# One decoder layer: the first input chunk in fp32, the decay as a background job, and a turned order of the down projection

## The chip, the cores and the metric

The kernel runs on one core of a Trainium2 chip. The metric is the device time of one execution in microseconds (us), smaller is better. The engines are TensorE (PE, matmuls; PEld is its load of weights), VectorE (DVE), ScalarE (ACT), GpSimd (POOL) and SyncE (SP), which issues most DMAs. Each engine works through its own instruction stream in order; streams meet at semaphores.

## The reference, cut to what matters

One layer of a hybrid decoder on 256 tokens of width 2048, all in float32:

```python
h = rms_norm(x, ln1)
proj = h @ w_in              # gdn q|k|v, beta, decay, z, moba q|k|v, gate a, gate b
y_a = gated_deltanet(...) @ w_branch_a     # conv of 4, silu, delta rule with decay, * silu(z)
y_b = moba_attention(rope(q_b), rope(k_b), v_b) @ w_branch_b
x = x + (sigmoid(gate_a) * y_a + sigmoid(gate_b) * y_b) @ w_out
u = causal_dwconv(rms_norm(x, ln2) @ w_up, ffn_conv, bias)
x = x + (silu(u_gate) * u_val) @ w_down
return rms_norm(x, final_norm)
```

The decay is `g = -exp(a_log) * softplus(a_logit + dt_bias)`, cumulated along the tokens for each of 8 heads; `beta` is a sigmoid of its own column. `rms_norm` is `x * rsqrt(mean(x^2)) * ln1`. The kernel leaves out the factor of the token (`rsqrt`, in the kernel `R1`) until after the matmul, since it is constant over the contraction, and multiplies only `ln1` in beforehand.

## The kernel before, in words

**Matmuls in split form.** Most matmuls take operands in fp32r. A float32 operand is split into a high part (`wh`, `hh`: a cast on ACT, line 118) and a low part (`wl`, `hl`: the rest, a subtraction on DVE, line 115), and three products are summed: high by high, high by low, low by high. `fetch` gets a raw block of 128x2048 weights by DMA into one of four buffers `wraw`; `load_w` splits it in pieces of 1024 columns into `wh` and `wl`, two buffers each. `chunk` computes two 128-row blocks of a projection against all tokens in a tile `ps` of PSUM (`mmt`, three buffers, tag "mm"); `by_token` computes the transposed form, tokens on the partitions, with 512 columns to a matmul, in two such tiles. Small things use another five PSUM buffers (`sdt`, tag "sd").

**The start.** `xs`, the transposed input, and the first two weight blocks `wq` come in 16 pieces of 256 KB, `xs` before `wq` in each pair (lines 250 and 251). For each quarter of the contraction, `scaled` multiplies `xs` by `ln1` and splits it into `hc` (`hh` on ACT, line 216; `hl` on DVE, line 217), the weights are split, and 4 x 3 matmuls for each of two blocks go to `ps_q0`: 96 in all. Then follow the fetches of `wbd`, `bd`, the second chunk's weights `raws` and the constant tables, the squares of `xs` (three of four on POOL), the 32 matmuls `ps_bd` for beta and decay, and `rstd`, which gives `R1` from a sum over the partitions by two fp32 matmuls with `ones` (tile `R`).

**The decay.** From `ps_bd` and `R1` a chain of some 25 small instructions on 16 partitions (lines 310 to 349, DVE with ACT's sigmoid and exp between) makes `beta`, the cumulated decay `gc`, its split and `rem`. `columns` transposes these and `R1` on PE into `pt_cols` and copies them to `cols`.

**The loop over groups.** For four groups of two heads, three chunks (q, k, v) are computed, and each goes through `conv4`: `join` multiplies `ps` by `R1` on DVE (line 212), which frees the PSUM tile, then come the four taps of the convolution and a silu. Groups 0 and 2 also compute `ps_z` for four heads by token. Then the group's `gdn` generator is appended to `bg`. Four groups of attention follow (`moba`), then the gates, the two branch projections, the output projection, the up projection in 44 chunks (`ps_up`) and the down projection.

**Order.** `main_mm` adds 108 to a counter for a matmul of 256 columns and 215 for one of 512; whenever it has reached `EVERY` = 1700, `tick` advances each generator in `bg` by one step. So background work is written between the main matmuls. A planner with a simulated timeline then sets the order of each engine's instructions: what is written first has priority, but work that it expects to be ready earlier can go ahead. After the third group of attention, `bg` is ticked until one job is left, and the pool `g` of the delta rule is closed.

**The down projection.** Eight PSUM banks `pd[i][n]` collect 128 tokens x 512 columns each; they take the banks that the up projection's tiles held. For each of 40 blocks of the contraction the eight are visited in `order`; the first visit begins with four transposes of `x1` (line 814). The last four blocks are done accumulator by accumulator, each followed by the final norm.

Of the kernel before, what the change touches and what calls it, by code (L numbers as in the profile page):

```python
# [11 lines left out]
F32 = mybir.dt.float32  # L12
# [68 lines left out]
def layer_kernel(ctx: ExitStack, tc: tile.TileContext, xT, pos, cst, csel, ceye, vec, convw, ffw, bdv,  # L81
# [30 lines left out]
            tick()  # L112

    def low(hi, lo, src, eng=None):
        (eng or dve).tensor_tensor(lo, src, hi.bitcast(F32), op=ALU.subtract)  # L115

    def split(hi, lo, src):
        act.copy(hi, src)  # L118
        low(hi, lo, src)

    def three(ah, al, bh, bl):
        return [(ah, bh), (ah, bl), (al, bh)]

    def fetch(src, n=2048):
        raw = wpool.tile([P, 2048], F32, name="wraw", tag="wraw", bufs=4)
# [3 lines left out]
    def parts(o=0):  # L129

        return [wpool.tile([P, 2048 + 128], F32R, name=t, tag=t)[:, o:o + 2048] for t in ("wh", "wl")]

    def load_w(src, n=2048, into=None, piece=1024, raw=None):
        raw = raw or fetch(src, n)
        wh, wl = into or parts()
        for o in range(0, n, piece):
            split(wh[:, o:o + piece], wl[:, o:o + piece], raw[:, o:o + piece])
        return wh[:, :n], wl[:, :n]


# [98 lines left out]

    xs = g.tile([P, KD, T], F32, name="xs")  # L240

    wq = []
    for b in range(2):
        raw = wpool.tile([P, 2048], F32, name="wraw", tag="wraw", bufs=4)
        wq.append((raw, *parts()))
    for i in range(4):
        s = slice(4 * i, 4 * i + 4)
        for b in range(2):
            h = slice(4 * i + 2 * b, 4 * i + 2 * b + 2)
            sp.dma_start(xs[:, h, :], xT[:, h, :])  # L250
            sp.dma_start(wq[b][0][:, 512 * i:512 * i + 512], w_gdn[b][:, 512 * i:512 * i + 512])
    ps_q0 = mmt("ps_gdn")
    for i in range(4):
        scaled(xs[:, 4 * i:4 * i + 4, :], ln1v, 4 * i, hh, hl)
        for b in range(2):
# [55 lines left out]
    dve.tensor_tensor(z0, z0, R1[:16, :], op=ALU.mult)
    act.activation(beta, z0, AF.Sigmoid)
    dve.tensor_scalar(z0, z0, bd[:, 0:1], None, op0=ALU.add)
    nz = g.tile([16, T], F32, name="nz")
    dve.scalar_tensor_tensor(nz, z0, -1.0, z0, op0=ALU.mult, op1=ALU.min)
    ez = g.tile([16, T], F32, name="ez")
    act.activation(ez, nz, AF.Exp)
    ea = fk.tile([16, 1], F32, name="ea")
    act.activation(ea, bd[:, 1:2], AF.Exp)
    den = g.tile([16, T], F32, name="den")  # L320
    dve.tensor_scalar(den, ez, 2.0, None, op0=ALU.add)
    dve.reciprocal(den, den)
    sv = g.tile([16, T], F32, name="sv")
    dve.tensor_tensor(sv, ez, den, op=ALU.mult)
    s2 = g.tile([16, T], F32, name="s2")
    dve.tensor_tensor(s2, sv, sv, op=ALU.mult)
    pv = g.tile([16, T], F32, name="pv")
    dve.tensor_scalar(pv, s2, 1.0 / 15, None, op0=ALU.mult)
    for n in (13, 11, 9, 7, 5, 3):
        dve.scalar_tensor_tensor(pv, pv, 1.0 / n, s2, op0=ALU.add, op1=ALU.mult)  # L330
    dve.scalar_tensor_tensor(pv, pv, 1.0, sv, op0=ALU.add, op1=ALU.mult)
    spv = g.tile([16, T], F32, name="spv")
    dve.tensor_scalar(spv, z0, 0.0, None, op0=ALU.max)
    dve.scalar_tensor_tensor(spv, pv, 2.0, spv, op0=ALU.mult, op1=ALU.add)
    gt = g.tile([16, T], F32, name="gt")
    dve.tensor_scalar(gt, spv, ea, -1.0, op0=ALU.mult, op1=ALU.mult)
    gc = fk.tile([16, T], F32, name="gc")
    for i in range(2):
        dve.tensor_tensor_scan(gc[:, i * P:(i + 1) * P], ones[:16, :], gt[:, i * P:(i + 1) * P], 0.0,
                               op0=ALU.mult, op1=ALU.add)  # L340
    gch = fk.tile([16, T], F32R, name="gch")
    gcl = fk.tile([16, T], F32R, name="gcl")
    split(gch, gcl, gc)
    selr = fk.tile([16, 8, P], F32R, name="selr")
    dve.tensor_copy(selr, self_)
    sint = fk.tile([48, T], F32, name="sint")
    cost = fk.tile([48, T], F32, name="cost")
    rem = cost[:16, :P]
    dve.tensor_scalar(rem, gc[:, :P], gc[:, P - 1:P], -1.0, op0=ALU.subtract, op1=ALU.mult)
    n1.close()  # L350

    ya = fk.tile([P, H, T], F32, name="ya")
# [58 lines left out]
        dve.tensor_scalar(cost, cost, -2.0, 1.0, op0=ALU.mult, op1=ALU.add)  # L411


    def columns():
# [4 lines left out]
        pe.transpose(pt[:, 32:48], rem, ident[:16, :16])  # L419
        for i in range(2):  # L420
            pe.transpose(pt[:, 80 + 16 * i:96 + 16 * i], R1[:16, i * P:(i + 1) * P], ident[:16, :16])
        cols = fk.tile([P, 7, 16], F32, name="cols")
        dve.tensor_copy(cols.rearrange("p a b -> p (a b)"), pt[:, :112])
        return cols

    def conv4(t, ps, b0):
        un = g.tile([P, 2, T], F32, name="un", bufs=1)
# [180 lines left out]
    def pair(w, i):  # L608
        return [w[2 * i], w[2 * i + 1]]

    for gr in range(4):
        h0 = 2 * gr
        kq = g.tile([P, 2, 2, T], F32, name="kq", bufs=1)
        v = g.tile([P, 2, T], F32, name="v", bufs=1)
        for a, t in enumerate((kq[:, 1], kq[:, 0], v)):
            if gr == a == 0:
                ps = ps_q0
            else:
                ps = chunk(pair(w_gdn, 3 * gr + a), hc, KD, "gdn", *([raws] if (gr, a) == (0, 1) else []))
# [57 lines left out]
    for gr in range(4):  # L677
        h0 = 2 * gr
        qk = []
        for a in range(2):  # L680
            ps = chunk(pair(w_moba, 2 * gr + a), hc, KD, "moba")
            t = m.tile([P, 2, T], F32, name=f"qk{a}")
            join(t, ps, R1b)
            qk.append(t)
        if gr % 2 == 0:
            ps = by_token(w_mv[2 * gr:2 * gr + 4], hc, KD, "ps_v")
            v4 = m.tile([P, 2, 2 * T], F32, name="v_")
            for i in range(2):
                act.mul(v4[:, i, :], ps[i], cols[:, 5 + i, 0:1])
        v = v4[:, :, (gr % 2) * T:(gr % 2 + 1) * T]  # L690
        bg.append(moba(h0, *qk, v))
        if gr == 2:
            while len(bg) > 1:
                tick()
            gdn_st.close()
            y_st = ExitStack()
            gp = y_st.enter_context(tc.tile_pool(name="gp", bufs=1, side="right", reuse_waits="tile"))


    gts = gp.tile([P, 2, 8, 512], F32, name="gts")  # L700
# [232 lines left out]
```

## Time and profile before

| | |
|---|---|
| device time, median of 3 runs | 1508.7 us (1507.93 to 1508.71) |
| profiled execution, device time | 1508.24 us |
| its span, first to last instruction | 1506.5 us |
| PE busy | 1482.6 us (98%), 8507 matmuls |
| PEld busy | 1305.9 us (87%) |
| DVE busy | 991.3 us (66%) |
| ACT busy | 743.4 us (49%) |
| POOL busy | 172.4 us (11%) |
| the chain that ended last | PE 92%, DVE 4%, ACT 1%, DMA 1% |
| DMA | 276.84 MB, mean 184 GB/s |

The span is the time between the first and the last instruction on the chip; the device time holds 1.74 us more around it. "Busy" is the time in which at least one instruction of an engine was running, as the profiler records it; a matmul's recorded length includes its way through the array, so successive matmuls overlap, and the pace of PE is read from the distance between their starts. An fp32 matmul is recorded as two matmuls.

### The profile page before, as it was taken

The numbers are of one execution on the slowest core, as the hardware profiler recorded it, in microseconds if no ns is written. First come the engines' busy times: TensorE is split into PE (matmuls) and PEld (weight loads), VectorE is DVE, ScalarE is ACT, GpSimd is POOL, SyncE is SP. The second block draws the span as 40 slices with busy tenths as digits, with TensorE's granted clock in tenths as the row PEclk, the third lists the DMA queues.
The fourth block names the chain that finished last, engine by engine and source line by source line (L and its number), as shares of the span: only waits on it lengthen the run. The fifth ranks groups of instructions, "written<-read, shape, count | busy, mean of one in ns | idle before, by whom it ended". The sixth has DMA issues, their size and how long they took to land.

```text
span 1506.5 us, 21027 instructions
## 1 busy us (share of the span) xinstructions
PE 1482.6 (98%) x8507; PEld 1305.9 (87%) x8507; DVE 991.3 (66%) x1413; ACT 743.4 (49%) x997; POOL 172.4 (11%) x130
## 2 busy tenths in 40 slices
PE   7999999999999999999999999999999999999997
PEld 7899899998988888888888888888888888888886
DVE  8888668796655444666667677676776765555554
ACT  5565454435474444434455555554555554444444
POOL 3011001141203000000101212112111120000000
PEclk9999999999999999999999999999999999999999
DMA  8355444444445555546555555555555544555552
GB/s 312 141 198 190 163 154 157 149 169 147 154 154 174 193 194 194 193 177 249 186 208 196 184 188 188 196 196 182 188 189 196 196 177 162 195 195 194 195 196 84
DMA packets 43329, 276.84 MB, mean 184 GB/s; under 512 B 5248, under 2 KB 6736, under 8 KB 11104
## 3 DMA queue, kind: packets, MB, share of 16 engines
q1 hardware_dynamic: 41408, 270.98, 50.2%
q0 software_dynamic: 960, 2.36, 0.5%
q10 hardware_dynamic: 864, 2.16, 0.4%
q8 instruction: 66, 1.08, 0.3%
q14 instruction: 31, 0.25, 0.0%
HBM read 271.68 MB, written 3.80 MB: 183 GB/s over the span
## 4 chain that ended last, share of the span: by engine, by line
PE 92%; DVE 4%; ACT 1%; DMA 1%; issue 1%; SPq 0%; DVEq 0%; ACTq 0%; POOLq 0%
PE ps_up L108 32%; PE pd L96 16%; PE ps_gate L108 10%; PE ps_gdn L108 9%; PE ps_wo L108 6%; PE ps_br L108 6%; PE ps_moba L108 3%; PE ps_z L108 3%; PE ps_v L108 3%; DVE wl L115 2%; ACT wh L118 1%; DMA xs<-in_xT 1%; PE g L96 1%; PE pu L564 1%; PE py L558 1%
## 5 line engine op out<-in xcount | busy, mean ns | idle before, releaser
L115 DVE TENSOR_TENSOR wl<-wraw,wh 128x1024 fp32r<-128x1024 f32 (+1 forms) x504 | 603.3, 1233 | 275.4 <-ACT wh L118 274.8
L118 ACT CAST wh<-wraw 128x1024 fp32r<-128x1024 f32 (+1 forms) x504 | 500.1, 1039 | 411.3 <-PE ps_up L108 117.3
L108 PE MATMUL ps_up<-h,wh 128*128 128x512 f32 x1408 | 488.6, 390 | 0.0
L108 PE MATMUL ps_up<-h,wl 128*128 128x256 f32 x1408 | 397.0, 282 | 0.0
L108 PEld LDWEIGHTS ps_up<-h,wh 128*128 128x128 f32 x1408 | 264.2, 188 | 55.4
L108 PEld LDWEIGHTS ps_up<-h,wl 128*128 128x128 f32 x1408 | 266.1, 189 | 0.1
L108 PE MATMUL ps_gate<-wh,hc 128*128 128x512 f32 x512 | 156.0, 391 | 0.0
L108 PE MATMUL ps_gdn<-hc,wh 128*128 128x256 f32 x768 | 142.5, 287 | 8.8 <-ACT wh L118 6.0
L96 PE MATMUL pd<-wl,ah 128*128 128x512 f32 x336 | 130.8, 389 | 0.0
L96 PE MATMUL pd<-wh,al 128*128 128x512 f32 x336 | 130.8, 389 | 0.0
L108 PEld LDWEIGHTS ps_gdn<-hc,wh 128*128 128x128 f32 x768 | 121.7, 194 | 9.9 <-ACT wh L118 6.0
L800 POOL TENSOR_TENSOR acts<-sg,cvf 128x256 f32<-128x256 f32 x44 | 80.7, 1833 | 423.4 <-ACT sg L799 423.4
L108 PEld LDWEIGHTS ps_gate<-wh,hc 128*128 128x128 f32 x512 | 95.8, 188 | 19.7
L108 PE MATMUL ps_gdn<-hc,wl 128*128 128x256 f32 x384 | 110.2, 287 | 1.1 <-DVE wl L115 1.1
L794 ACT ACTIVATE cvf<-unf,ffv 128x256 f32<-128x256 f32 x88 | 48.2, 595 | 104.4 <-DVE unf L212 104.4
L796 DVE SCALAR_TENSOR_TENSOR cvf<-unf,ffv,cvf 128x254 f32<-128x254 f32 (+1 forms) x176 | 77.3, 480 | 32.1 <-ACT cvf L794 31.8
L108 PE MATMUL ps_gate<-wl,hc 128*128 128x512 f32 x256 | 97.1, 391 | 0.0
L108 PE MATMUL ps_moba<-hc,wh 128*128 128x256 f32 x512 | 93.1, 282 | 0.0
L96 PE MATMUL pd<-wh,ah 128*128 128x512 f32 x336 | 92.8, 391 | 0.0
L108 PE MATMUL ps_wo<-mc,wh 128*128 128x512 f32 x256 | 89.0, 390 | 0.4 <-ACT wh L118 0.4
L118 ACT CAST ah<-acts 128x256 fp32r<-128x256 f32 x44 | 17.9, 406 | 128.0 <-PE pd L96 118.3
L108 PEld LDWEIGHTS ps_moba<-hc,wh 128*128 128x128 f32 x512 | 78.7, 188 | 0.2
(420 smaller groups left out, 1881.5 us busy)
## 6 DMA issues: line engine op xcount, KB each, us to landing
wraw<-in_w_up SPq DMA_DIRECT2D x88, 1024.0 KB, 4.8
wraw<-in_w_dn SPq DMA_DIRECT2D x44, 1024.0 KB, 4.8
wraw<-in_w_gate SPq DMA_DIRECT2D x32, 1024.0 KB, 4.8
wraw<-in_w_gdn SPq DMA_DIRECT2D x22, 1024.0 KB, 4.9
wraw<-in_w_moba SPq DMA_DIRECT2D x16, 1024.0 KB, 5.0
wraw<-in_w_o SPq DMA_DIRECT2D x16, 1024.0 KB, 4.8
wraw<-in_w_z SPq DMA_DIRECT2D x8, 1024.0 KB, 4.8
wraw<-in_w_mv SPq DMA_DIRECT2D x8, 1024.0 KB, 4.8
```

Of the source, the lines that this page charges most:

```text
L96: pe.matmul(ps, a, b, start=(start and i == 0), stop=(stop and i == n - 1), **kw)
L108: pe.matmul(ps, a, b, start=start, stop=stop, skip_group_check=True)
L115: (eng or dve).tensor_tensor(lo, src, hi.bitcast(F32), op=ALU.subtract)
L118: act.copy(hi, src)
L558: pe.matmul(py[:, p], ats[p], Tm[:, p], start=True, stop=True)
L564: pe.matmul(pu[:, p], Y[:, p, :], odd(U)[:, p], start=True, stop=True)
L794: act.activation(t[:, j, :], un[:, j, :], AF.Identity, scale=w[:, 2:3], bias=w[:, 3:4])
L796: dve.scalar_tensor_tensor(t[:, j, d:], un[:, j, :T - d], w[:, 2 - d:3 - d], t[:, j, d:], op0=ALU.mult, op1=ALU.add)
L800: pool.tensor_tensor(acts[:, c, :], sg, t[:, 1, :], op=ALU.mult)
```

## The change

The start fetches weights before `xs` in each pair. The first chunk is no longer split: the raw weights are multiplied in place by `ln1` on DVE and multiplied with the raw `xs` in fp32, 32 matmuls (not counted by `main_mm`). Ten fp32 matmuls on `ones` stand ahead of everything on PE. `scaled` still makes `hc`, now for the second chunk on, and the second chunk is written directly behind it, before the squares, `ps_bd` and `R1`. All four squares are on ACT, their sums on DVE. The decay's chain becomes a generator `decay`, appended to `bg` behind the second chunk's `conv4` and finished before `gdn(0)` starts; `R1`'s columns get transposes of their own. The pool of the delta rule is closed after the attention loop, once the last `gdn` is done. In the down projection the pairs of accumulators are visited in another order.

```diff
     def low(hi, lo, src, eng=None):
-        (eng or dve).tensor_tensor(lo, src, hi.bitcast(F32), op=ALU.subtract)
+        return (eng or dve).tensor_tensor(lo, src, hi.bitcast(F32), op=ALU.subtract)
...
-            split(wh[:, o:o + piece], wl[:, o:o + piece], raw[:, o:o + piece])
+            lows.append(split(wh[:, o:o + piece], wl[:, o:o + piece], raw[:, o:o + piece]))
...
+    warm = sdt("warm")
+    for i in range(10):
+        pe.matmul(warm[:, :P], ones, ones, start=True, stop=True)
+    wq = [wpool.tile([P, 2048], F32, name="wraw", tag="wraw", bufs=4) for _ in range(2)]
+    for i in range(4):
+        for b in range(2):
+            h = slice(4 * i + 2 * b, 4 * i + 2 * b + 2)
+            sp.dma_start(wq[b][:, 512 * i:512 * i + 512], w_gdn[b][:, 512 * i:512 * i + 512])
+            sp.dma_start(xs[:, h, :], xT[:, h, :])
+    ps_q0 = mmt("ps_gdn")
     for i in range(4):
         s = slice(4 * i, 4 * i + 4)
         for b in range(2):
-            h = slice(4 * i + 2 * b, 4 * i + 2 * b + 2)
-            sp.dma_start(xs[:, h, :], xT[:, h, :])
-            sp.dma_start(wq[b][0][:, 512 * i:512 * i + 512], w_gdn[b][:, 512 * i:512 * i + 512])
-    ps_q0 = mmt("ps_gdn")
+            w = r3(wq[b], P)[:, s]
+            dve.tensor_tensor(w, w, ln1v[:, s, None].to_broadcast([P, 4, P]), op=ALU.mult)
+        for b in range(2):
+            for k in range(4 * i, 4 * i + 4):
+                pe.matmul(ps_q0[:, b], r3(wq[b], P)[:, k], xs[:, k], start=(k == b == 0), stop=(k == KD - 1),
+                          skip_group_check=True)
     for i in range(4):
         scaled(xs[:, 4 * i:4 * i + 4, :], ln1v, 4 * i, hh, hl)
-        for b in range(2):
-            raw, wh, wl = (t[:, 512 * i:512 * i + 512] for t in wq[b])
-            split(wh, wl, raw)
-            for k in range(4):
-                a = 4 * i + k
-                main_mm(ps_q0[:, b], r3(wh, P)[:, k], hh[:, a], a == b == 0, False)
-                main_mm(ps_q0[:, b], r3(wh, P)[:, k], hl[:, a], False, False)
-                main_mm(ps_q0[:, b], r3(wl, P)[:, k], hh[:, a], False, a == KD - 1)
+    raws = [fetch(w) for w in (w_gdn[2], w_gdn[3])]
     wbd = g.tile([P, KD, 16], F32, name="wbd")
     sp.dma_start(wbd, w_bd)
     bd = fk.tile([16, 2], F32, name="bd")
     sp.dma_start(bd, bdv)
-    raws = [fetch(w) for w in (w_gdn[2], w_gdn[3])]
...
+    ps_k0 = chunk([w_gdn[2], w_gdn[3]], hc, KD, "gdn", raws)
...
-        if i < 3:
-            pool.tensor_tensor(sq[i], xv, xv, op=ALU.mult)
-        else:
-            act.activation(sq[i], xv, AF.Square)
-    pool.tensor_tensor(sq[0], sq[0], sq[1], op=ALU.add)
-    dve.tensor_tensor(sq[2], sq[2], sq[3], op=ALU.add)
+        act.activation(sq[i], xs[:, 4 * i:4 * i + 4, :], AF.Square)
+    dve.tensor_tensor(sq[0], sq[0], sq[1], op=ALU.add)
+    with tc.issue_after(lows[2].ins):
+        dve.tensor_tensor(sq[2], sq[2], sq[3], op=ALU.add)
...
+    def decay():          # the former lines 311 to 349, with tiles in buffers of pool m
+        ...               # z0 * R1, sigmoid, + bias, min
+        yield
+        ...               # exp, reciprocal
+        yield
+        ...               # the series
+        yield
+        ...               # softplus, gt, two scans to gc
+        yield
+        split(gch, gcl, gc)
+        dve.tensor_scalar(rem, gc[:, :P], gc[:, P - 1:P], -1.0, op0=ALU.subtract, op1=ALU.mult)
+        yield from wait(2)
         pt = sdt("pt_cols")
...
+    def rms_columns():
+        pt = sdt("pt_rms")
         for i in range(2):
-            pe.transpose(pt[:, 80 + 16 * i:96 + 16 * i], R1[:16, i * P:(i + 1) * P], ident[:16, :16])
+            pe.transpose(pt[:, 16 * i:16 * i + 16], R1[:16, i * P:(i + 1) * P], ident[:16, :16])
...
+            if gr == 0 and a < 2:
+                ps = (ps_q0, ps_k0)[a]
             else:
...
             conv4(t, ps, 8 * a + h0)
+            if gr == 0 and a == 1:
+                bg.append(decay())
         if gr == 0:
-            cols = columns()
+            rms_columns()
...
-        bg.append(gdn(h0, kq, v))
+        while gr == 0 and bg:
+            tick()
+        gdns.append(gdn(h0, kq, v))
+        bg.append(gdns[-1])
...
-        if gr == 2:
-            while len(bg) > 1:
-                tick()
-            gdn_st.close()
+    while gdns[-1] in bg:
+        tick()
+    gdn_st.close()
...
-    order = [(1, 2), (1, 3)] + [(0, n) for n in range(4)] + [(1, 0), (1, 1)]
+    order = [(1, 2), (1, 3), (0, 2), (0, 3), (1, 0), (1, 1), (0, 0), (0, 1)]
```

## Rows read from the trace of the kernel before

**Rows 1.** The waits of PE: instruction, releaser, us in total, times, longest.

```profile
PE ps_gdn L108 <- ACT wh L118: 6.0, 1, 6.0
...
PE pd L814 <- DVE unf L210: 1.7, 1, 1.7
...
PE u L570 <- DVE U L565: 0.8, 1, 0.8
...
PE pT L662 <- DVE s__4149 L656: 0.4, 1, 0.4
```

**Rows 2.** The chain of waits in order: start us, us, engine, tile, line, count.

```profile
27.65 3.74 PE ps_bd L96 x32
31.75 0.86 PE R L96 x4
32.61 21.95 PE ps_gdn L108 x188
...
61.59 5.72 PE ps_z L108 x24
67.31 0.79 PE ssq L460 x8
```

**Rows 3.** The timeline, PE's start: start us, us, instruction, idle before.

```profile
9.40 0.63 PE L108 MATMUL ps_gdn<-hc,wh 128*128 128x256 f32 x2
...
9.83 0.41 PE L108 MATMUL ps_gdn<-hc,wl 128*128 128x256 f32 x1
...
16.40 0.58 PE L108 MATMUL ps_gdn<-hc,wh 128*128 128x256 f32 x1 [1.88 <-DVE hc L217]
```

**Rows 4.** Stretches of PE: from:to, length, busy, count, granted clock, DMA share, GB/s.

```profile
6.00:12.70 6.70, 6.02 (x25) 1.00 0.99 319
...
16.10:22.90 6.80, 5.42 (x23) 0.50 1.00 379
```

**Rows 5.** The timeline, DVE and ACT, 11 to 30 us.

```profile
11.73 4.62 DVE L217 SCALAR_TENSOR_TENSOR hc<-xs,vc,hc 128x256 fp32r<-128x256 f32 x2
...
22.75 0.87 DVE L217 SCALAR_TENSOR_TENSOR hc<-xs,vc,hc 128x256 fp32r<-128x256 f32 x2
...
24.68 0.68 DVE L115 TENSOR_TENSOR wl<-wraw,wh 128x512 fp32r<-128x512 f32 x1
...
27.25 1.23 DVE L115 TENSOR_TENSOR wl<-wraw,wh 128x1024 fp32r<-128x1024 f32 x1 [0.42 <-ACT wh L118]
...
26.17 3.90 ACT L118 CAST wh<-wraw 128x1024 fp32r<-128x1024 f32 x4 [6.23 <-PE ps_gdn L108]
```

**Rows 6.** The timeline, ACT and the DMA issues on SP.

```profile
8.81 0.62 ACT L118 CAST wh<-wraw 128x512 fp32r<-128x512 f32 x1 [1.44 <-DMA wraw<-in_w_gdn]
...
11.67 0.33 SPq L251 DMA_DIRECT2D wraw<-in_w_gdn  x1
...
14.50 0.34 SPq L126 DMA_DIRECT2D wraw<-in_w_gdn  x1
```

**Rows 7.** DMA issues at 11.67 and at 14.50: count, KB, us to landing.

```profile
wraw<-in_w_gdn SPq DMA_DIRECT2D x1, 256.0 KB, 6.1
...
wraw<-in_w_gdn SPq DMA_DIRECT2D x1, 1024.0 KB, 6.2
```

**Rows 8.** The timeline, the decay's chain: its first step and `pt_cols`.

```profile
35.40 0.41 DVE L311 TENSOR_TENSOR z<-z,R 16x256 f32<-16x256 f32 x1
...
54.59 0.23 PE L417 MATMUL pt_cols<-ct,gc 16*128 16x16 f32 x1
```

**Rows 9.** The timeline, PE in `ps_z`.

```profile
61.59 0.70 PE L108 MATMUL ps_z<-wh,hc 128*128 128x512 f32 x2 [0.72 <-DVE un L212]
```

**Rows 10.** The timeline, the first pass of the down projection.

```profile
1256.35 0.68 DVE L210 TENSOR_TENSOR unf<-ps_up,unf 128x512 f32<-128x512 f32 x1
...
1257.09 0.66 PE L814 MATMUL pd<-identb,x 128*128 128x128 f32 x4 [1.74 <-DVE unf L210]
...
1258.28 0.60 PE L814 MATMUL pd<-identb,x 128*128 128x128 f32 x4
```

More of the change, by code (lines that the diff above doesn't have):

```diff
@@ L114, in low @@
     def low(hi, lo, src, eng=None):
-        (eng or dve).tensor_tensor(lo, src, hi.bitcast(F32), op=ALU.subtract)
+        return (eng or dve).tensor_tensor(lo, src, hi.bitcast(F32), op=ALU.subtract)
     def split(hi, lo, src):
         act.copy(hi, src)
-        low(hi, lo, src)
+        return low(hi, lo, src)
     def three(ah, al, bh, bl):
         return [(ah, bh), (ah, bl), (al, bh)]
+    lows = []
     def fetch(src, n=2048):
@@ L240, in layer_kernel @@
     xs = g.tile([P, KD, T], F32, name="xs")
-    wq = []
-    for b in range(2):
-        raw = wpool.tile([P, 2048], F32, name="wraw", tag="wraw", bufs=4)
-        wq.append((raw, *parts()))
+    warm = sdt("warm")
[8 more added lines that the diff above has]
+    ps_q0 = mmt("ps_gdn")
     for i in range(4):
@@ L307, in layer_kernel @@
     beta = fk.tile([16, T], F32, name="beta")
-    z0 = g.tile([16, T], F32, name="z0")
+    sint = fk.tile([48, T], F32, name="sint")
+    z0 = sint[:16]
     act.copy(z0, s[32:48, :])
     dve.tensor_tensor(z0, z0, s[:16, :], op=ALU.add)
[L311 to L317, printed above, removed]
-    ea = fk.tile([16, 1], F32, name="ea")
[L319 to L336, printed above, removed]
+    ea = fk.tile([16, 1], F32, name="ea")
     gc = fk.tile([16, T], F32, name="gc")
-    for i in range(2):
-        dve.tensor_tensor_scan(gc[:, i * P:(i + 1) * P], ones[:16, :], gt[:, i * P:(i + 1) * P], 0.0,
-                               op0=ALU.mult, op1=ALU.add)
     gch = fk.tile([16, T], F32R, name="gch")
     gcl = fk.tile([16, T], F32R, name="gcl")
-    split(gch, gcl, gc)
     selr = fk.tile([16, 8, P], F32R, name="selr")
     dve.tensor_copy(selr, self_)
-    sint = fk.tile([48, T], F32, name="sint")
     cost = fk.tile([48, T], F32, name="cost")
     rem = cost[:16, :P]
-    dve.tensor_scalar(rem, gc[:, :P], gc[:, P - 1:P], -1.0, op0=ALU.subtract, op1=ALU.mult)
+    cols = fk.tile([P, 7, 16], F32, name="cols")
     n1.close()
@@ L411, in rotary @@
         dve.tensor_scalar(cost, cost, -2.0, 1.0, op0=ALU.mult, op1=ALU.add)
-    def columns():
+    def decay():
+        nz, ez, den, sv, s2, pv, spv, gt = (m.tile([16, T], F32, name=n, tag=t) for n, t in (
+            ("nz", "qk0"), ("ez", "qk0"), ("den", "qk1"), ("sv", "qk1"), ("s2", "s_"), ("pv", "s_"),
+            ("spv", "pT_"), ("gt", "pT_")))
+        dve.tensor_tensor(z0, z0, R1[:16, :], op=ALU.mult)
+        act.activation(beta, z0, AF.Sigmoid)
+        dve.tensor_scalar(z0, z0, bd[:, 0:1], None, op0=ALU.add)
+        dve.scalar_tensor_tensor(nz, z0, -1.0, z0, op0=ALU.mult, op1=ALU.min)
+        yield
+        act.activation(ez, nz, AF.Exp)
+        act.activation(ea, bd[:, 1:2], AF.Exp)
+        dve.tensor_scalar(den, ez, 2.0, None, op0=ALU.add)
+        dve.reciprocal(den, den)
+        dve.tensor_tensor(sv, ez, den, op=ALU.mult)
+        dve.tensor_tensor(s2, sv, sv, op=ALU.mult)
+        yield
+        dve.tensor_scalar(pv, s2, 1.0 / 15, None, op0=ALU.mult)
+        for n in (13, 11, 9, 7, 5, 3):
+            dve.scalar_tensor_tensor(pv, pv, 1.0 / n, s2, op0=ALU.add, op1=ALU.mult)
+        dve.scalar_tensor_tensor(pv, pv, 1.0, sv, op0=ALU.add, op1=ALU.mult)
+        yield
+        dve.tensor_scalar(spv, z0, 0.0, None, op0=ALU.max)
+        dve.scalar_tensor_tensor(spv, pv, 2.0, spv, op0=ALU.mult, op1=ALU.add)
+        dve.tensor_scalar(gt, spv, ea, -1.0, op0=ALU.mult, op1=ALU.mult)
+        for i in range(2):
+            dve.tensor_tensor_scan(gc[:, i * P:(i + 1) * P], ones[:16, :], gt[:, i * P:(i + 1) * P], 0.0,
+                                   op0=ALU.mult, op1=ALU.add)
+        yield
+        split(gch, gcl, gc)
+        dve.tensor_scalar(rem, gc[:, :P], gc[:, P - 1:P], -1.0, op0=ALU.subtract, op1=ALU.mult)
+        yield from wait(2)
         pt = sdt("pt_cols")
@@ L419, in columns @@
         pe.transpose(pt[:, 32:48], rem, ident[:16, :16])
+        dve.tensor_copy(cols[:, :5].rearrange("p a b -> p (a b)"), pt[:, :80])
+    def rms_columns():
+        pt = sdt("pt_rms")
         for i in range(2):
-            pe.transpose(pt[:, 80 + 16 * i:96 + 16 * i], R1[:16, i * P:(i + 1) * P], ident[:16, :16])
-        cols = fk.tile([P, 7, 16], F32, name="cols")
-        dve.tensor_copy(cols.rearrange("p a b -> p (a b)"), pt[:, :112])
-        return cols
+            pe.transpose(pt[:, 16 * i:16 * i + 16], R1[:16, i * P:(i + 1) * P], ident[:16, :16])
+        dve.tensor_copy(cols[:, 5:].rearrange("p a b -> p (a b)"), pt[:, :32])
     def conv4(t, ps, b0):
@@ L609, in pair @@
         return [w[2 * i], w[2 * i + 1]]
+    gdns = []
     for gr in range(4):
@@ L615, in layer_kernel @@
         for a, t in enumerate((kq[:, 1], kq[:, 0], v)):
-            if gr == a == 0:
-                ps = ps_q0
+            if gr == 0 and a < 2:
+                ps = (ps_q0, ps_k0)[a]
             else:
-                ps = chunk(pair(w_gdn, 3 * gr + a), hc, KD, "gdn", *([raws] if (gr, a) == (0, 1) else []))
+                ps = chunk(pair(w_gdn, 3 * gr + a), hc, KD, "gdn")
             conv4(t, ps, 8 * a + h0)
+            if gr == 0 and a == 1:
+                bg.append(decay())
         if gr == 0:
-            cols = columns()
+            rms_columns()
         if gr % 2 == 0:
@@ L691, in layer_kernel @@
         bg.append(moba(h0, *qk, v))
-        if gr == 2:
-            while len(bg) > 1:
-                tick()
-            gdn_st.close()
-            y_st = ExitStack()
-            gp = y_st.enter_context(tc.tile_pool(name="gp", bufs=1, side="right", reuse_waits="tile"))
+    while gdns[-1] in bg:
+        tick()
+    gdn_st.close()
+    y_st = ExitStack()
+    gp = y_st.enter_context(tc.tile_pool(name="gp", bufs=1, side="right", reuse_waits="tile"))
     gts = gp.tile([P, 2, 8, 512], F32, name="gts")
```

2 lines of the change are left out of this document (removed).

## The prediction

> **What bounds the kernel now.** I read the page first, then the list of what TensorE (PE) waited for, the chain of waits, and the timeline of the few places that these two name. On the page the reader is to see that PE is busy almost all of the span and that the chain that ended last is nearly all PE. So a step pays only where it changes the start or the end of the unbroken PE stream, closes one of the stream's holes, or changes its matmuls. The list of PE's waits [rows 1] shows how few holes there are: 6.0 us at the very start, 1.7 us at the first transposes of the down projection (`pd`), 0.7 us in `ps_z` [rows 9], and six others of 0.4 to 0.8 us (0.8 + 0.7 + 0.7 + 0.5 + 0.4 + 0.4 = 3.5 us). The chain [rows 2] shows the start: the first chunk's matmuls last to 27.65, the 32 matmuls of `ps_bd` and the sum of `R` follow, and from 32.61 the next chunks stand back to back.
>
> How the first 27.65 us pass is in the timeline. No matmul before 5.97. Then matmuls of 256 columns are spaced 0.215 us (two in 0.43, 9.40 to 9.83 [rows 3]), where 188 of them take 21.95 us, 0.117 each, later [rows 2]. A ratio of nearly two is the clock: PE runs at 1.2 GHz there and at 2.4 GHz later. The granted clock stands at 1.00 for 6 to 12.7 us and at 0.50 for 16.1 to 22.9 [rows 4]; for the first of the two I go by the spacing. At 16.40 PE had stood 1.88 us for `hc` [rows 3], behind VectorE (DVE), whose two scalings of `xs` took 4.62 us where two take 0.87 otherwise [rows 5]; GpSimd was busy with squares of `xs` in that stretch.
>
> [...] By the recorded grant PE would be at full clock from its first matmul, the ten added matmuls would raise nothing, and the start would be worth 5.0 us; by the spacing it is 4.6.
>
> **The first chunk.** Removed: 96 matmuls on split operands, eight casts on ScalarE (ACT) and eight subtractions on DVE for the split. Added: eight scalings on DVE of 128x512, for which the subtraction of the same shape stands (0.68 us, [rows 5]), and 32 matmuls in fp32 of 256 columns. Their price is in `R`: its first sum is two such matmuls, recorded as four, in 0.86 us [rows 2], so 0.43 us each at full clock, 0.86 at the low one. The 32 cost 13.8 us against 96 x 0.117 = 11.2: 2.6 us more work for PE, which the waits must pay for.
>
> When can they run? The 16 pieces of 256 KB keep their number; each pair is swapped, so weights take the `xs` places. The fourth piece was in at 8.81, which ended an ACT wait of 1.44 us; the last landed 6.1 us after its issue at 11.67, at 17.8 [rows 6, 7]. After the change the fourth piece is `xs` of blocks 2 and 3, and the program needs it for the third matmul. So PE does two matmuls on arrival (about 5.3), stands until 8.8, and has 30 left: 30 x 0.43 = 12.9, to 21.7 at best. From there PE is slower than the data (17.8 plus one scaling of 0.7).
>
> The clock is the unknown. The ten fp32 matmuls on `ones` have 128 columns, half of `R`'s, so 0.43 us each at the low clock: 4.3 us, about 1.0 to 5.3, ahead of any data, at no cost. But the pause before 8.8 follows, 2 us or more, like the one of 1.88 us before 16.40, and after that one the grant was 0.50 [rows 3, 4]. Best case: full clock from 8.8, end at 21.7. Worst likely case: PE slow from 8.8 as long as it was from 16.4 to 22.9 [rows 3, 4], 6.5 us, half of it lost: 25.0. I take 23.0, nearer the best, since PE has worked 6 us before the pause and works on without a hole after it.
>
> The second chunk must be ready then. Its first raw block, issued at 14.50, landed 6.2 us later, at 20.7 [rows 6, 7]; it now goes ahead of `wbd`, so 20.3 to 20.7. One cast (four in 3.90 us, so 1.0) and one subtraction (1.23) [rows 5] give the first half at 22.6 to 22.9. Its other input, `hc`, needs 16 scalings on DVE (0.44 each, 7.0 us), which with the eight new ones make 12.5 us of DVE from 4.3 on, and GpSimd's squares, which stretched them, are gone to ACT (four of about 1.0 us, in idle ACT). So the second chunk begins at 23.0 in the place of 27.65: a gain of 4.6 us, bounds 2.6 (25.0) and 5.0 (22.6). `ps_bd` and `R` (27.65 to 32.61, 4.96 us) only move behind this chunk and cost the same. The fetches of `raws` pass `wbd` and `bd` on SP's queue; both small tables are wanted only after the second chunk. The third chunk's weights need the slots of the first, free at 23.0, where the last of its subtractions began at 24.68 [rows 5]: no later.
>
> **Decay as a background job.** Before, the joins of the first three chunks stood behind the decay's chain on DVE: `z0` times `R1` at 35.40, `pt_cols` at 54.59 [rows 8], and the second join let `ps_z` wait 0.72 us at 61.59 [rows 9]. Afterwards the joins need `R1` alone. `R` ends near 23.0 + 11.2 + 5.0 = 39.2, `R1` is usable 2.8 us later as before (32.61 to 35.40), at 42.0, and the third chunk runs to 39.2 + 11.2 = 50.4. Two joins and one set of taps take some 5 us of DVE, so `ps_z` finds its buffers free: gain 0.7, bounds 0 and 0.7. The decay's own instructions are the same; ACT may load a table or two more, which is idle time there. I add 0.5 us, bounds 0 and 2, for holes that DVE's new order may leave in front of a split of weights.
>
> **Turned order of the down projection.** PE finishes two accumulators and then stands 1.74 us for `pd0_0`, whose bank the last chunk's join still reads (1256.35, [rows 10]). Turned, this pair comes last: six accumulators 1.2 us apart (1257.09 to 1258.28) stand before it, four more than now, 4.8 us of cover for 1.7 of wait. The pairs put before it take the banks of the last chunk but one and but two, joined a chunk earlier and more. Gain 1.7, bounds 0 (if the planner holds the join still longer) and 1.7. The closing of the pool for the branch A work moves behind the loop; its last job had ended before the old place by my count of ticks (48 of some 49), so nothing.
>
> **Sum.** 1508.24 (profiled execution) - 4.6 - 0.7 + 0.5 - 1.7 = 1501.7. That execution is 0.46 under the median of 1508.7 and inside the runs' spread, so 1501.7 stands for the median too. The likeliest case's own range: gains of 5.0 + 0.7 + 1.7 with no new hole give 1500.8; 2.6 + 0 + 1.7 less 1 give 1504.9.
>
> **Rivals.**
> *DVE bunches its work.* If its order puts the 16 scalings of `xs` behind the last scaling of weights (18.5), they end at 25.5 and the subtraction at 26.7; the second chunk starts there, gain 0.95 in place of 4.6: 1505.4. For it: DVE is the busiest engine beside PE at the start. Against: in the trace it alternates the two kinds piece by piece.
>
> *`pt_cols` in the middle of `ps_z` (slower).* The decay's job sends its transposes to PE at its seventh step. By the tick count (1700 units, 108 a matmul of 256 columns, 215 of 512) that is 7 matmuls of 0.24 us (24 in 5.72, [rows 2]) into `ps_z`: 50.4 + 1.7 = 52.1. The decay's chain took 54.59 - 35.40 = 19.2 us; from 42.0 it ends at 61.2. If PE's order follows the code, PE stands 9.1 us: 1510.8. It decides from the point where the transposes stand within 4.3 us of `ps_z`'s start (18 matmuls): then the whole gain is gone. Against: the planner places work by when it expects it ready; `gdn`'s `ssq`, written after all of `ps_z`, ran inside it (67.31, [rows 2]).
>
> *The clock stays down.* If the whole first chunk runs at 1.2 GHz, 30 x 0.86 = 25.8 from 8.8 is 34.6, 7.0 later than before: 1513.3. It loses from an end of the chunk at 29.6 on. Against: PE had full clock after 6.7 us of work with only short holes before [rows 4].
>
> *Other holes close too.* The six others go with the new interleaving: 1501.7 - 3.5 = 1498.2. They could as well grow.
>
> **Chances.** Forecast 0.66, bunched DVE 0.14, `pt_cols` 0.06, clock 0.04, other holes 0.10. Range 1497.5 to 1506.0: it leaves out the two slow rivals, part of the bunched case and the tail below, 0.18 in all. 0.2% is 3.0 us, about what can be told from no change: faster means under 1505.7. Forecast, closed holes and two thirds of the bunched case: 0.85 faster. The rest of that and half of the `pt_cols` case: 0.08 same. Slower 0.07.
>
> **What would show it.** The first chunk as 64 records ending near 23; the second chunk from there without a hole; `ps_z` without its wait; `pd` without its 1.7 us; the later stretches of the same length. It is wrong if PE's stretch of matmuls at the low clock reaches far past 12, if DVE's last scaling of `xs` lies after 21, or if PE waits for `pt_cols`.

## The result and the profile after

The changed kernel takes 1498.91 us (median of 4, 1497.78 to 1499.27) against 1508.32 for the kernel before (median of 4 beside it): a ratio of 0.9935, 95% interval 0.9923 to 0.9947. The forecast was 1501.7, with 1497.5 to 1506.0 as its range. The gain, 9.4 us, is larger than the 6.5 to 7 forecast.

The page of the profiled execution, its span, PE's line and the granted clock in 40 slices:

```profile
span 1497.3 us, 20988 instructions
...
PE 1485.1 (99%) x8495; PEld 1308.3 (87%) x8495; DVE 986.6 (66%) x1415; ACT 738.6 (49%) x990; POOL 164.3 (11%) x126
...
PEclk9999999999999999999999999999999999999999
```

PE is busy 2.5 us longer than before in a span 9.2 us shorter. Of the 2.5 us, 2.0 are not there when the changed kernel is run again (1483.1 us): the first profile has a stretch at the low clock, told of at the end. The fp32 matmuls are a little more work, and the holes are fewer. What PE waited for, in full (instruction, releaser, us in total, times, longest), answers to [rows 1]:

```profile
PE warm L247 <- POOL ones L147: 1.0, 1, 1.0
PE ps_gdn L108 <- DVE wl L115: 0.7, 1, 0.7
PE ps_wo L108 <- DVE wl L115: 0.7, 1, 0.7
PE ps_v L108 <- DVE wl L115: 0.6, 1, 0.6
PE ps_wo L108 <- ACT wh L118: 0.4, 1, 0.4
PE ps_gdn L264 <- DMA xs<-in_xT: 0.4, 1, 0.4
PE ps_gate L108 <- DVE qk L214: 0.3, 1, 0.3
```

The 6.0 us at the start, the wait of `ps_z`, the two of `u` and those of `pT` are gone, and so is the 1.7 us of `pd`. The start on PE's timeline, to be held against [rows 3]:

```profile
1.00 4.63 PE L247 MATMUL warm<-ones 128*128 128x128 f32 x20 [1.00 <-POOL ones L147]
5.70 1.68 PE L264 MATMUL ps_gdn<-xs,wraw 128*128 128x256 f32 x4
7.73 13.22 PE L264 MATMUL ps_gdn<-xs,wraw 128*128 128x256 f32 x60 [0.35 <-DMA xs<-in_xT]
20.64 0.55 PE L108 MATMUL ps_gdn<-hc,wh 128*128 128x256 f32 x2
21.90 0.38 PE L108 MATMUL ps_gdn<-hc,wl 128*128 128x256 f32 x1 [0.72 <-DVE wl L115]
```

The ten warm matmuls (20 records) fill the time before data. The fp32 matmuls start at 5.70, with four records in 1.68 us. They stand 0.35 us for the second piece of `xs`, and run on at 0.22 us a record from 7.73, at full clock. From 20.64 on the second chunk is ready but for its low part: the 0.72 us at 21.90. Where that comes from is on ACT's and DVE's timeline, where [rows 5] stood:

```profile
17.88 1.67 DVE L219 SCALAR_TENSOR_TENSOR hc<-xs,vc,hc 128x256 fp32r<-128x256 f32 x4
...
19.54 1.99 ACT L118 CAST wh<-wraw 128x1024 fp32r<-128x1024 f32 x2 [0.63 <-DMA wraw<-in_w_gdn]
...
20.62 2.36 DVE L115 TENSOR_TENSOR wl<-wraw,wh 128x1024 fp32r<-128x1024 f32 x2 [1.08 <-ACT wh L118]
```

The cast waits 0.63 us for the raw block to land, the subtraction for the cast, PE for the subtraction. DVE had been done with `xs` for 1.1 us. From 21.90 the chain runs without a break through what stands in [rows 2] and on through `ps_z`:

```profile
21.90 11.23 PE ps_gdn L108 x94
33.13 3.63 PE ps_bd L96 x32
36.76 0.86 PE R L96 x4
37.62 11.20 PE ps_gdn L108 x96
49.05 21.99 PE ps_z L108 x96
```

For the comparison of runs, the first `ps_z` matmul marks the end of the start. Read off PE's timelines, in us:

| kernel | first `ps_z` | from there to first `ps_br` | first to last matmul of `pd` | median, runs |
|---|---|---|---|---|
| before | 55.14 | 526.78 | 245.13 | 1508.32, 4 |
| changed, first profile | 48.98 | 525.77 * | 243.16 | 1498.91, 4 |
| changed, run again | 49.22 | 524.16 | 243.15 | 1497.67, 5 |
| changed, old order in `pd` | 49.19 | 524.18 | 245.13 | 1499.69, 5 |
| changed, no warm matmuls | 49.20 | 524.15 | 243.15 | 1499.49, 5 |
| changed, split first chunk | 51.09 | 524.87 | 243.15 | 1499.59, 5 |
| changed, decay at once | 48.79 | 524.30 | 243.15 | 1497.44, 5 |
| changed, old closing of the pool | 48.78 | 525.75 * | 243.16 | 1498.88, 5 |
| changed, squares on GpSimd | 56.72 | 524.13 | 243.15 | 1503.29, 5 |
| changed, second chunk late | 50.18 | 524.22 | 243.15 | 1498.57, 5 |
| changed, raw blocks in halves | 48.47 | 524.24 | 243.15 | 1496.76, 4 |
| the same, and paired blocks | 48.59 | 524.14 | 243.15 | 1497.01, 4 |
| before, squares off GpSimd | 51.29 | 528.27 * | 245.10 | 1504.62, 6 |
| the same, and warm matmuls | 50.92 | 526.51 | 245.10 | 1503.52, 5 |

A star marks a profile with 3.4 us at the low clock near 215 us, some 1.6 us in that stretch; it is told of at the end. Between the first `ps_br` and the first `pd` all are alike: 670.97 to 670.99 us for the kernel before, the changed one and all others. So the gain has three places, read from before and the changed kernel run again, which has no star: 5.9 us in the start, 2.6 in the middle, 2.0 in `pd`; 10.5 of the 10.6 by which their spans differ (1506.5 and 1495.9).

### The profile page after: what moved, and what is told of

Its sections match the earlier page's. It is cut to its first block, busy times and chain, and to the rows that moved or that the text cites. A ratio compares the mean times of both kernels' runs of the same rounds, so it can differ in the third digit from the quotient of the medians.

```text
span 1497.3 us, 20988 instructions
## 1 busy us (share of the span) xinstructions
PE 1485.1 (99%) x8495; PEld 1308.3 (87%) x8495; DVE 986.6 (66%) x1415; ACT 738.6 (49%) x990; POOL 164.3 (11%) x126
## 4 chain that ended last, share of the span: by engine, by line
PE 96%; DVE 2%; DMA 1%; ACT 0%; SPq 0%; issue 0%; DVEq 0%; ACTq 0%
PE ps_up L108 33%; PE pd L96 16%; PE ps_gate L108 12%; PE ps_gdn L108 8%; PE ps_wo L108 6%; PE ps_br L108 6%; PE ps_moba L108 5%; PE ps_z L108 3%; PE ps_v L108 3%; DMA wraw<-in_w_gdn 1%; DVE wl L115 1%; PE py L565 1%; PE pu L571 1%; PE g L96 1%; PE t L557 0%; DVE tm L535 0%
## 5 line engine op out<-in xcount | busy, mean ns | idle before, releaser
L115 DVE TENSOR_TENSOR wl<-wraw,wh 128x1024 fp32r<-128x1024 f32 x496 | 598.7, 1243 | 276.0 <-ACT wh L118 275.3
L118 ACT CAST wh<-wraw 128x1024 fp32r<-128x1024 f32 x496 | 495.2, 1046 | 398.8 <-PE ps_up L108 117.5
L108 PE MATMUL ps_gdn<-hc,wh 128*128 128x256 f32 x704 | 126.2, 281 | 0.0
L108 PEld LDWEIGHTS ps_gdn<-hc,wh 128*128 128x128 f32 x704 | 108.0, 188 | 0.7
L108 PE MATMUL ps_gdn<-hc,wl 128*128 128x256 f32 x352 | 99.1, 281 | 0.7 <-DVE wl L115 0.7
L96 PE MATMUL pd<-wh,ah 128*128 128x512 f32 x336 | 86.6, 391 | 0.0
```

Of the source, the lines that this page charges most:

```text
L96: pe.matmul(ps, a, b, start=(start and i == 0), stop=(stop and i == n - 1), **kw)
L108: pe.matmul(ps, a, b, start=start, stop=stop, skip_group_check=True)
L115: return (eng or dve).tensor_tensor(lo, src, hi.bitcast(F32), op=ALU.subtract)
```

## The experiments

**The changed kernel again.**

> The changed kernel once more, unedited, on the same chip as the three beside it. Its first profile had 3.4 us at the low clock at 215 us, in the middle of dense work, which cost some 1.5 us. If that belongs to single executions, this profile lacks it and its stretch from the first ps_z matmul to the first ps_br matmul is 524.2 us in place of 525.8, time near 1497.5; if it belongs to the kernel, it stands at the same place again, 1499.

1497.67 us (1497.05 to 1498.13), and 524.16 in the middle. The first reading was right: the low clock came with single executions, and the changed kernel without it is near 1497.7.

**Old order of the down projection.**

```diff
-    order = [(1, 2), (1, 3), (0, 2), (0, 3), (1, 0), (1, 1), (0, 0), (0, 1)]
+    order = [(1, 2), (1, 3)] + [(0, n) for n in range(4)] + [(1, 0), (1, 1)]
```

> The changed kernel with the old order of accumulators in the down projection. Theory (a hole in PE's stream is closed and nothing takes its place): PE stands 1.7 to 2.0 us at the first transposes of the third accumulator again, and the whole kernel is 2.0 us slower than the changed one, 1500.9 us. Rival (the join is late in any order, the wait only moves): less than 0.5 us, 1499.0 to 1499.4.

The wait is back, at its old length:

```profile
PE pd L826 <- DVE unf L212: 1.7, 1, 1.7
```

The stretch of `pd` is 245.13 again, to the hundredth what it was before: the order is worth 1.97 us, and this run is 2.0 us above the changed kernel run again (on another chip). In the changed kernel the pair that waits comes last, and by then its join is long done (start us, us, engine, line):

```profile
1247.99 0.60 PE L826 MATMUL pd<-identb,x 128*128 128x128 f32 x4
...
1249.13 0.60 PE L826 MATMUL pd<-identb,x 128*128 128x128 f32 x4
1249.15 0.68 DVE L212 TENSOR_TENSOR unf<-ps_up,unf 128x512 f32<-128x512 f32 x1
...
1252.54 0.60 PE L826 MATMUL pd<-identb,x 128*128 128x128 f32 x4
```

The join reads the bank at 1249.15 (line 212); the seventh accumulator is wanted at 1252.54 only.

**No warm matmuls.**

```diff
-    warm = sdt("warm")
-    for i in range(10):
-        pe.matmul(warm[:, :P], ones, ones, start=True, stop=True)
```

> The changed kernel without the ten matmuls on ones. Theory (the clock is low until PE has worked, whatever the recorded grant says for the first microseconds): fp32 matmuls spaced 0.43 us per record from 5.7 to about 12 us, the first chunk ends 2.3 to 3.4 us later (23 to 24 in place of 20.6), time 1501 to 1502.5. Rival (the recorded grant of 1.00 is right, the ten matmuls raise nothing): no difference, 1498.9.

```profile
5.61 2.07 PE L261 MATMUL ps_gdn<-xs,wraw 128*128 128x256 f32 x4 [5.61 <-DVE wraw L258]
8.04 14.10 PE L261 MATMUL ps_gdn<-xs,wraw 128*128 128x256 f32 x60 [0.35 <-DMA xs<-in_xT]
```

The pace is low at first (four records in 2.07 us, where after ten warm matmuls four profiles have 1.13), and the first chunk ends at 22.14 in place of 20.95. Yet `ps_z` comes at 49.20, where the changed kernel has 48.98 and 49.22: with warm matmuls PE had to stand for the second chunk's weights until 21.9 in any case. So the theory holds for the pace, and in this profile it fails for the price, 0.2 us at most. But this profile is of the shortest of the five runs, 1497.71. The others go up to 1500.23, and the median, 1499.49, is 2.0 us above that of the run with the decay at once (1497.44), made beside it on the same chip, whose edit changed nothing. At the median the warm matmuls look worth some 2 us, then, not far below the 2.3 to 3.4 expected; where the longer runs lost them, no profile shows.

**Split first chunk.** The 96 split matmuls are back; warm matmuls, squares and the order of the fetches stay.

```diff
-            w = r3(wq[b], P)[:, s]
-            dve.tensor_tensor(w, w, ln1v[:, s, None].to_broadcast([P, 4, P]), op=ALU.mult)
-        for b in range(2):
-            for k in range(4 * i, 4 * i + 4):
-                pe.matmul(ps_q0[:, b], r3(wq[b], P)[:, k], xs[:, k], ...)
+            raw, wh, wl = (t[:, 512 * i:512 * i + 512] for t in (wq[b], *qp[b]))
+            split(wh, wl, raw)
+            ...      # three pe.matmul for each k, as in the kernel before
```

> The changed kernel with the first chunk in split form again (96 matmuls instead of 32 in fp32), all else kept: warm matmuls, weights ahead of xs, all squares on ACT. Theory (fp32 pays because its operands are ready after one short scaling, while the split needs a cast, a subtraction and the scaled xs one after another): the chunk ends at 21.5 to 23 in place of 20.6, time 1500 to 1501.5. Rival (the warm clock and the squares taken off GpSimd did it; fp32 only adds 2.6 us of PE work): the chunk ends at 20.6 or before, time 1496.5 to 1498.9.

The chain of the split version, where the second chunk begins:

```profile
21.64 1.06 ACT wh L118
22.73 1.24 DVE wl L115
24.00 11.24 PE ps_gdn L108 x94
```

It begins at 24.00, 2.1 us later than in the changed kernel, after the same cast and subtraction. What held the cast is on ACT's timeline:

```profile
21.64 3.89 ACT L118 CAST wh<-wraw 128x1024 fp32r<-128x1024 f32 x4 [0.31 <-PE ps_gdn L266]
```

ACT is busy with the first chunk's casts and scalings and the squares until 21.3, and then stands 0.31 us until a matmul of the first chunk (line 266) is done: the split first chunk holds both buffers of `wh`, and one must come free. In the kernel before, ACT stood 6.23 us ahead of the same cast, and it was again a matmul that ended it [rows 5]. In fp32 the first chunk uses neither buffer, and the cast waits for the landing alone. The theory's sign and size hold: fp32 is worth 1.9 us of the start. The rival fails, though a large part of the gain is there without fp32.

**Squares back on GpSimd.**

```diff
-        act.activation(sq[i], xs[:, 4 * i:4 * i + 4, :], AF.Square)
-    dve.tensor_tensor(sq[0], sq[0], sq[1], op=ALU.add)
+        if i < 3:
+            pool.tensor_tensor(sq[i], xv, xv, op=ALU.mult)
+        else:
+            act.activation(sq[i], xv, AF.Square)
+    pool.tensor_tensor(sq[0], sq[0], sq[1], op=ALU.add)
```

> The changed kernel with three of the four squares of xs, and one sum, back on GpSimd. Theory (two-input work of GpSimd holds VectorE up: two scalings of xs took 4.62 us before where two take 0.87): scalings of weights are held up too, the first chunk ends 1 to 3 us later than 20.6, time 1 to 2 us above the changed kernel. Rival (VectorE has slack here, since TensorE's fp32 work and the landing of the second chunk's weights set the end of the start): less than 0.5 us.

The largest effect of all: 1503.29 us, 5.6 above the changed kernel run again beside it, and the first `ps_z` at 56.72, later than before the change. DVE's timeline, then GpSimd's:

```profile
11.21 4.59 DVE L219 SCALAR_TENSOR_TENSOR hc<-xs,vc,hc 128x256 fp32r<-128x256 f32 x2
15.72 2.38 DVE L261 TENSOR_TENSOR wraw<-wraw,vc 128x512 f32<-128x512 f32 x1
18.02 0.87 DVE L219 SCALAR_TENSOR_TENSOR hc<-xs,vc,hc 128x256 fp32r<-128x256 f32 x2
```

```profile
11.12 1.91 POOL L297 TENSOR_TENSOR sq<-xs 128x1024 f32<-128x1024 f32 x1 [0.72 <-DMA xs<-in_xT]
13.12 2.40 POOL L300 TENSOR_TENSOR sq<-sq,sq 128x1024 f32<-128x1024 f32 x1
15.48 2.07 POOL L297 TENSOR_TENSOR sq<-xs 128x1024 f32<-128x1024 f32 x1
```

Two scalings of `xs` take 4.59 us, one scaling of weights 2.38, about as long as GpSimd's sums and squares of 128x1024 last. Each ends 0.3 to 0.6 us behind one of those (13.3, 15.80 and 18.10, against 13.03, 15.52 and 17.55). With GpSimd idle two take 0.87. PE pays for it at once:

```profile
8.42 4.92 PE L264 MATMUL ps_gdn<-xs,wraw 128*128 128x256 f32 x20 [1.51 <-DMA xs<-in_xT]
18.16 11.29 PE L264 MATMUL ps_gdn<-xs,wraw 128*128 128x256 f32 x40 [4.82 <-DVE wraw L261]
```

4.82 us for one scaled piece of weights, where the changed kernel has no wait like it, and the 40 records behind it take 11.29 us instead of 8.8, because the clock had fallen while PE stood (from:to, length, busy, count, granted clock, DMA share, GB/s):

```profile
16.20:23.03 6.83, 4.87 (x12) 0.50 1.03 379
```

So some 2.5 us of the 7.5 by which the first `ps_z` is later than in the changed kernel run again are the clock's. I had expected 1 to 2 us in all. The profiled execution is the longest of the five (1505.19).

*A rule of the Trainium skill.* SBUF — State Buffer, section "Who interferes with whom", says that a DVE instruction with two inputs from SBUF contends with a GpSimd instruction that reads SBUF, that the ports they share are an exclusive lock, and that the order of issue decides which of the two waits. The ends above agree: these DVE instructions have two such inputs, and they end just behind GpSimd's.

**Before, with the squares off GpSimd; and with warm matmuls.** The same edit the other way round, in the kernel before, then also the ten matmuls.

> The kernel before with one part of the change alone: all four squares of xs on ScalarE and their first sum on VectorE, none on GpSimd. Theory from the run with the squares put back (GpSimd's two-input work held VectorE up, and this was the larger part of the start's cost): VectorE's scalings of xs take 0.9 us for two throughout, the first ps_z matmul comes 2.5 to 4 us before 55.1, time 1504.5 to 1506. Rival (the split form itself, through cast, subtraction and scaled xs, sets the start, so fp32 is needed): less than 1 us.

> The same with the ten warm matmuls on ones as well. Theory (split matmuls that run at 0.215 us each up to 12 us now run at 0.117): 0.5 to 1.5 us more than the squares alone. Rival (operands arrive too late for TensorE's pace to matter, as without the warm matmuls in the changed kernel, where 0.2 us was lost): less than 0.3 us more.

1504.62 us, ratio 0.9972 (0.9960 to 0.9984), the first `ps_z` 3.9 us earlier; with warm matmuls 1503.52 and another 0.4 us. So the squares alone give two thirds of the start's 5.9 us. The medians of these two differ by 1.1 us, as expected for the second, but three of the first's runs, the profiled one among them, have a mean granted clock of 0.997 and are at least 1.0 us above its other three (0.998 and 0.999). The start itself gained 0.4, less than the 0.5 to 1.5 expected; its profile still has 2.8 us of waits for casts. The rest of the start's gain is fp32: the changed kernel has its first `ps_z` at 51.09 with the first chunk split and at 49.22 with it in fp32. The new order of fetches and the second chunk's new place added nothing while the first chunk was split (50.92 and 51.09).

**The decay at once.** All steps of the decay are written ahead of the joins, as before the change; its tiles stay in the buffers of pool `m`.

```diff
     gdns = []
+    bg.append(decay())
+    while bg:
+        tick()
...
-            if gr == 0 and a == 1:
-                bg.append(decay())
```

> The changed kernel with the decay's chain run through at once before the joins, as before the change, instead of as a background job. Theory: the joins stand behind some 19 us of the chain, ps_z waits for its second buffer again, 0.7 to 1.1 us slower, 1499.6 to 1500.0. Rival (the planner fills the time, PE is never kept waiting): within 0.3 us of the changed kernel.

1497.44 us: no difference, and no wait in `ps_z`. The theory failed. DVE's timeline shows the first join ahead of the decay's first step although it is written behind it:

```profile
40.89 0.69 DVE L214 TENSOR_TENSOR un<-ps_gdn,R 128x512 f32<-128x512 f32 x1
41.50 0.41 DVE L393 TENSOR_TENSOR sint<-sint,R 16x256 f32<-16x256 f32 x1
```

In the kernel before, that join stood directly behind the decay's last step (line 349):

```profile
54.15 0.25 DVE L349 TENSOR_SCALAR cost<-gc 16x128 f32<-16x128 f32 x1
54.33 0.67 DVE L212 TENSOR_TENSOR un<-ps_gdn,R 128x512 f32<-128x512 f32 x1
```

What differs in the code is where the tiles lie. Before, the decay's tiles were in pool `n1`, and `un`, which the join writes, is in pool `g`, which gets the memory of `n1` when that is closed. I read the 54.33 as a wait for that memory. No run here put the tiles back, so this is argued, not shown; shown is that the background job is not what freed the joins.

**Old closing of the pool.**

```diff
-    while gdns[-1] in bg:
-        tick()
-    gdn_st.close()
+        if gr == 2:
+            while len(bg) > 1:
+                tick()
+            gdn_st.close()
```

> The changed kernel with the closing of the delta rule's pool, and the ticking ahead of it, back inside the attention loop after the third group. Theory of the prediction (nothing is left to tick there, so it changes nothing): the stretch from the first ps_z matmul to the first ps_br matmul stays at 524.2 us. Rival (this is what closed the holes of the middle, 526.8 us before the change): it returns to 526 or more, 1.7 us slower.

525.75 in the middle, with the low clock at the same place as in the changed kernel's first profile (525.77): no difference, as the prediction said.

**Second chunk late.** Its line goes back into the loop, behind the first `conv4`.

> The changed kernel with the second chunk written back at its old place, in the loop behind the first conv4, so that squares, ps_bd and R1 are written before it again. What is asked: which part shortened the stretch from the first ps_z to the first ps_br matmul from 526.8 to 524.2 us, where the decay's place, the pool's closing, the split and the warm matmuls have been ruled out. Theory (the place of the second chunk, through the planner's order of what follows): 526 or more again, time 1499 to 1500. Rival (something else): 524.2 again, and the time within 1 us of the changed kernel's 1497.7.

524.22 in the middle: not the cause either. The start is 1.0 us longer: two sums of the squares (DVE, 1.23 us each) then come ahead of the chunk's first subtraction, which begins at 21.72 in place of 20.84.

**Raw blocks in halves; and paired blocks.**

```diff
-    raws = [fetch(w) for w in (w_gdn[2], w_gdn[3])]
+    raws = []
+    for w in (w_gdn[2], w_gdn[3]):
+        raws.append(wpool.tile([P, 2048], F32, name="wraw", tag="wraw", bufs=4))
+        for o in (0, 1024):
+            sp.dma_start(raws[-1][:, o:o + 1024], w[:, o:o + 1024])
```

> The changed kernel with the second chunk's two raw blocks fetched in halves of 1024 columns. Theory (the start now ends where the second chunk's first block has landed, been cast and subtracted; TensorE stands about 0.7 us there): the first cast starts about 1.3 us earlier, the second chunk's stream begins at 20.7 to 21.0 in place of 21.9, 1.0 us faster than the changed kernel beside it. Rival (TensorE's own fp32 work or the scaling of xs sets it): less than 0.3 us.

> The changed kernel with the raw blocks fetched in halves, and the first chunk's matmuls ordered so that each pair of contraction blocks is used for both weight blocks before the next pair. Theory (after the halves TensorE's own work from the first data on sets the start, and it stands 0.6 to 1.4 us for the second piece of xs): two fp32 matmuls fill that pause, first ps_z 0.6 to 0.9 us earlier than with the halves alone (48.5), time 1496.0. Rival (the second chunk's weights bind again at once): less than 0.3 us.

1496.76 us against 1497.67 beside it, 0.9 us; ratio to before 0.9920 (0.9906 to 0.9933). It beats both kernels, though against the changed one the step is small: its longest run (1497.28) lies above one of the other's five. The second chunk follows the first without a wait:

```profile
8.09 13.22 PE ps_gdn L264 x60
21.31 11.20 PE ps_gdn L108 x96
```

So the weights' landing was the bound. With the blocks paired as well, nothing more: the pause for `xs` (1.4 us with the halves alone) is filled, but PE then waits 1.3 us for the scaling of the other block's weights.

## Why the prediction was right, step by step

The total was within its range, and its sign and its three places were right. The start and the middle were mis-sized, both to the same side, and that the total stayed inside is partly luck: run again, at 1497.67, the kernel is only 0.2 us above the range's lower bound.

**The first chunk, 4.6 us forecast, 5.8 measured** (27.65 to 21.90; 5.5 in the run again, with 22.12), outside the bound of 5.0. A gap of 0.36 us behind `ps_bd` closed as well, which makes 6.2 and 5.9 at the first `ps_z`. The step that failed is the pause. I took the landing of the fourth piece, 8.8, from one execution; here it was in at 7.7, and the changed kernel and its edits in fp32 have PE going on between 7.3 and 8.4. The pause was 0.35 us, not 2 or more, and up to 1.5 us of pause (squares on GpSimd, at 8.42) did not lower the clock, which the forecast feared after [rows 3, 4]. The fear itself was not idle: in the split run PE stood 1.94 us before 9.29, and the granted clock was 0.50 from 8.30 to 15.12. So the chunk ended at 20.95, before my best case of 21.7. What then set the end was the other condition, the second chunk's weights, 21.9, where I had 22.6 to 22.9: the raw block landed at 19.5 instead of 20.3 to 20.7. The price of fp32 was right: 60 records in 13.22 us, 0.44 a matmul. One reading of [rows 1] was short: PE's list of the kernel before also has waits of 2.8 us for `hc` and 1.1 us for `wl`, beside the 6.0 us at the start and the six others. They lie inside the 27.65 us, so the sum is the same.

**What I gave no price.** GpSimd's squares stood in the prediction as a remark, with the 4.62 us of [rows 5] as the sign. They are the larger part of the step: moving them alone gives 3.9 us, and with all of the change but them the start is 1.6 us longer than before in the profile (56.72 against 55.14). That profile is of the longest run; by the medians, 5.6 us between that run and the kernel before beside it, of which the middle and `pd` are 4.6, it is some 1 us shorter. The prediction reckoned DVE at its undisturbed pace, but gave the move no term of its own; the sum came out because they move in the same change.

**The decay, 0.7 us forecast.** The wait of `ps_z` went as forecast, but not for the reason given. The allowance of 0.5 for new holes had the wrong sign: the middle shrank by 2.6 us, the wait included. Against the 0.7 + 0.8 + 0.7 + 0.5 + 0.4 = 3.1 us that left PE's list there (`ps_z`, two of `u`, two of `pT`), 0.6 (`ps_v`) and 0.3 (`ps_gate`) came. This is the rival of closing holes, in part, which I gave 0.10. Its cause is not settled: every edit of the changed kernel has 524.1 to 524.9 where no star stands, the kernel before and its edits 526.5 to 526.8, so it is in none of warm matmuls, split, squares, background job, pool closing or the second chunk's place; the decay's tiles in other buffers are what is left of the larger edits, untried. One of these waits does not hang on them: the split run has 0.8 us of `u` again, and 524.87. Nor is it the count that spaces the ticks: the 96 matmuls no longer counted were six full rounds of 16 (16 x 108 = 1728, over 1700), so what follows is ticked as before.

**The down projection, 1.7 forecast, 1.97 measured.** The hole went as the banks said, cover included.

**The rivals.** DVE did not bunch: it alternates, with its last scaling of `xs` ending at 19.5. `pt_cols` did not stop PE; the planner put it behind `ps_z` (columns of `R1` first):

```profile
49.00 0.29 PE L430 MATMUL pt_rms<-ct,R 16*128 16x16 f32 x2
...
74.37 0.23 PE L422 MATMUL pt_cols<-ct,gc 16*128 16x16 f32 x1
```

The clock did rise, and stayed up through the start.

## What to carry to other kernels

Before a step is credited with a gain, look at what else in the same stretch holds its engine: here the elementwise work of GpSimd stretched each DVE instruction up to five times, and moving it was worth more than the new matmul form. A landing time from one execution is one sample: bound a pause with several, and ask which condition binds next when the first is gone. Look also at which buffers a stage holds: here the next stage's cast had stood behind them. A wait on a PSUM bank at a change of phase can be closed by visiting the banks in the order in which they come free.

## What was not expected of the hardware

In two profiles of the changed kernel's family (the first one and the old closing) the granted clock fell to 0.50 at 215 us and stayed there for 3.4 us, in dense work; in the kernel before with the squares off GpSimd it did so at 212 us. In the run again it did not, with the same instructions. First the stretches of the first profile (length, busy, count, granted clock, DMA share, GB/s), then the same one of the run again:

```profile
212.20:215.06 2.86, 2.86 (x25) 1.00 0.86 301
215.06:218.47 3.41, 3.41 (x19) 0.50 0.13 55
218.47:221.90 3.43, 3.43 (x31) 1.00 0.00 0
```

```profile
215.06:218.47 3.41, 3.41 (x31) 1.00 0.15 62
```

In those 3.4 us 19 matmul records stand where the other run has 31. PE had no pause before; what it ran just ahead were short matmuls, eight of 64 columns, eight of one column, and four that use 16 rows:

```profile
212.19 1.00 PE L565 MATMUL py<-Tm,aq 128*128 128x64 f32 x8
213.03 1.00 PE L467 MATMUL ssq<-ones,sqq 128*128 128x1 f32 x8
213.96 0.38 PE L96 MATMUL bc_g<-gch,selr 16*128 16x256 f32 x1
```

It costs some 1.6 us. That would explain the two groups of the changed kernel's first four runs (1497.78, and 1498.76 to 1499.27). Only one of them was profiled, but the mean granted clock of every run is on record and agrees: 0.999 for the first, 0.997 for the other three. The old closing's runs divide in the same way: 1496.95 and 1497.76 at 0.998 and 0.999, 1498.88 to 1499.56 at 0.997. Several differences above are no larger, so they were read from stretches of the profile and not from medians alone.
